# Layer 0's experts take the context rows of four experts as one tile and the context units of both halves as one tile, and the first route and gather stand inside the routing stage

## The chip, the cores and the metric

One core of one Trainium2 chip runs the whole program. The metric is the device time of one execution in microseconds (us); lower is better. TensorE (PE) multiplies, VectorE (DVE) and ScalarE (ACT) split and move tiles, GpSimd (POOL) issues gathers and scatters, and SyncE (SP) issues nearly all other DMA transfers, in its program's order.

## The reference, cut to what matters

The model has two layers over 1024 latent tokens and 256 context tokens of width 1024. A layer has a mixer (layer 0 recurrent, layer 1 attention), an output projection, and then a mixture of 16 experts in which each expert chooses its tokens: 128 of the latents and, in layer 0 only, 32 of the context.

```python
def expert_choice_ffn(h, w_router, w_gate, w_up, w_down):
    B, T, _ = h.shape
    cap = CAP_FACTOR * T // N_EXPERTS
    aff = jax.nn.softmax((h @ w_router).astype(jnp.float32), axis=-1)
    g, idx = lax.top_k(jnp.swapaxes(aff, 1, 2), cap)
    ...
    xg = h[bidx, idx]
    hid = jax.nn.silu(jnp.einsum('becd,edf->becf', xg, w_gate)) * jnp.einsum('becd,edf->becf', xg, w_up)
    y = jnp.einsum('becf,efd->becd', hid, w_down) * g[..., None].astype(h.dtype)
    return jnp.zeros_like(h).at[bidx, idx].add(y)
```

## The kernel before, in words

Each layer ends in a `tail` (output projection by `mixed`, residual, router, and the choice of tokens) and then `experts`. Latent products are done in three fp32r matmuls (`mm3`, L138 to L140): each factor is split into a high part (ACT, L144) and a low part (DVE, L145). Weights come in chunks of 1 MB: `wc` is the raw chunk, `wch` and `wcl` its two parts. In layer 0 eight raw chunks fit: five in a ring, which earlier stages use for other weights too, and three spare ones; three pairs of `wch` and `wcl` fit. An expert uses twelve chunks: for each half of its 1024 hidden units two of w_gate and two of w_up (`gate_up`, called with q = 0 and 1), then four of w_down (`down`, q = 0 to 3).

Layer 0 does the context with the raw chunks in plain f32, four small matmuls at a time (`mm_context`, L1143). After the second chunk pair of a half it runs the half's context products (`cg<-wc,xct`, 16 instructions), and in `down` after q = 1 and after q = 3 the context products of two chunks (`cg<-wc,hct`, 8 instructions each). A raw chunk can be loaded over only after its context products. Ahead of the products, PE turns tiles by transposition: `xg` (latent rows, `prep`, L1195), `xgc` (32 context rows of this expert, L1203), `sil` (hidden units of a half, `turn`, L1266) and `hc` (context units of a half, L1272). ACT or DVE copy what was turned to `xct` and `hct`.

PE's order is set by hand; a scheduler orders the other engines by it. `rt_hot` and `rt_i` make the list of an expert's rows (`route`), POOL gathers them (`xg<-hl,rt_i`), and the results are added by a scatter (`xl<-ye,rt_i`). `pooled` and `gated` say how the low parts of a layer's first chunks are made: on POOL, or on DVE behind a small POOL instruction.

In `mixed`, `oc` are the mixer's rows, `owr` and `wo` the raw and split weights of the attention's output projection, `wr` the router's weights, `rg` three rows of modulation and gain for the router, `rx` the residual rows, and `m` and `nf` modulation rows. `wdr` are weights of layer 1, loaded early, and `fe` rows of layer 0's mixer.

Of the kernel before, what the change touches and what calls it, by code (L numbers as in the profile page):

```python
# [22 lines left out]
D = 1024  # L23
# [85 lines left out]

class Kernel:  # L110
# [7 lines left out]
    pooled, gated = (2, 0), (0, 2)  # L118
# [16 lines left out]
    def mm3(self, out, a, b, first, last, skip=False):  # L135

        mm = self.nc.tensor.matmul
        mm(out, a[0], b[0], start=first, stop=False, skip_group_check=skip)  # L138
        mm(out, a[0], b[1], start=False, stop=False, skip_group_check=skip)  # L139
        mm(out, a[1], b[0], start=False, stop=last, skip_group_check=skip)  # L140
# [137 lines left out]
    def mod_round(self, l, r, pool, psum, ptag, wtile=None, column=False, ctag="tp", width=2048, **small):  # L278
# [6 lines left out]
        for k in range(KT):  # L285
# [12 lines left out]
            yield 1.0 / per  # L298
# [593 lines left out]
    def router(self, l, i, pool, psum):  # L892
# [22 lines left out]
    def affinities(self, h, r, out, turned, wr, pool, psum):  # L915
# [167 lines left out]

    def top_context(self, aff, pool, psum):
# [67 lines left out]
    def experts(self, l, routes, hs, xs, m5s, ring, pool, psum):  # L1152
# [10 lines left out]

        def pick(e):

            picked[e] = self.route(e, *routes[0], pool, tp())
            xg = pool.tile([128, D], F32, name="xg", bufs=2)
            fetched = gather(hs[0], picked[e][0], xg)
            if early and self.gated[l]:
                one = pool.tile([128, 1], F32, name="one")  # L1170
                with self.tc.issue_after(fetched.ins):
                    nc.gpsimd.memset(one, 1.0)
                for raw, hi, lo in early:
                    nc.vector.scalar_tensor_tensor(lo, raw, one, hi, op0=OP.mult, op1=OP.subtract)
            xgc = None
            if two:
                if e == 0:
                    routes[1] = self.top_context(routes[1], pool, tp)
                xgc = pool.tile([32, D], F32, name="xgc", bufs=2)
                gather(hs[1], routes[1][0][:, e:e + 1], xgc)  # L1180
            return xg, xgc
# [7 lines left out]
        def prep(xg, xgc):  # L1189
# [9 lines left out]
            if not two:  # L1199
                return xt, None  # L1200
            p = tp()
            for k in range(KT):
                nc.tensor.transpose(p[:, 32 * k:32 * k + 32], xgc[:, 128 * k:128 * k + 128], self.ident[:32, :32])  # L1203
            xct = pool.tile([128, KT, 32], F32, name="xct", bufs=2)
            nc.scalar.activation(xct, p[:, :256].rearrange("p (k t) -> p k t", t=32), AF.Copy)
            return xt, xct
# [10 lines left out]
        def wide_gate_up(e, q, x, accs):  # L1217

            for m, w in enumerate((wg, wu)):
                _, hi, lo = early.pop(0) if early else wide_chunk(e, q, w)  # L1220
                for a in range(2):
                    k = 2 * q + a
                    for half in range(2):
                        o = slice(512 * half, 512 * half + 512)
                        self.mm3(accs[half][:, m], (x[0][0][:, k, :], x[0][1][:, k, :]), (hi[:, a, o], lo[:, a, o]),
                                 k == 0, k == KT - 1)

        def gate_up(e, half, q, x, acc, cg):
            xt, xct = x
            c = []  # L1230
            for m, w in enumerate((wg, wu)):
                c.append(early.pop(0) if early else gate_up_chunk(e, half, q, w))
# [5 lines left out]
            if q:  # L1238
                for kk in range(KT):
                    self.mm_context(cg, xct, [held[2 * (kk // 4) + m][0][:, kk % 4, :] for m in range(2)], kk)  # L1240
                held.clear()

        def both(acc):

            sc = pool.tile([64, 512], F32, name="sc", bufs=2)
            nc.scalar.activation(sc, acc[64:128, :], AF.Copy)
            nc.vector.tensor_add(sc, sc, acc[0:64, :])
            return sc

        def activate(acc, cg):  # L1250
# [3 lines left out]
            if not two:  # L1254
                return sil, None
            sc = both(cg)
            hc = pool.tile([64, 512], F32, name="hc", bufs=2)
# [841 lines left out]
```

## Time and profile before

| | |
|---|---|
| median of 3 runs | 3310.74 us (3307.7 to 3312.14) |
| profiled execution | 3311.28 us, span 3309.5 us |
| mean granted TensorE clock | 0.962 |
| layer 0 experts | about 1087 to 1884 us |
| layer 1 tail | about 2510 to 2680 us |
| layer 1 experts | about 2681 to 3245 us |

The span runs from the first to the last instruction, and the time has 1.8 us more around it. A stage counts where PE waits, or where it never waits: there, only less PE work helps. The mean busy share of a stage doesn't tell which of the two it is; the list of PE's waits does.

### The profile page before, as it was taken

How to read it: one execution, taken by the hardware profiler on the slowest of the kernel's cores; microseconds unless marked ns; L12 is line 12 of the kernel's file. 1: busy time of each engine (PE TensorE's matmuls, PEld its weight loads, DVE VectorE, ACT ScalarE, POOL GpSimd, SP SyncE). 2: the span in 40 equal slices, each digit the busy share in tenths (PEclk: the TensorE clock that was granted, in tenths of full speed). 3: DMA queues.
4: the chain of work that ended last, by engine and by line, in shares of the span. 5: the costliest groups of instructions: out<-in, count | busy, mean ns of one | idle time of the engine just before them, and what ended most of it. 6: DMA issues, size and time to landing. Idle time of an engine off the chain costs nothing.

```text
span 3309.5 us, 50386 instructions
## 1 busy us (share of the span) xinstructions
PE 3051.5 (92%) x19910; PEld 2382.1 (72%) x19910; DVE 2264.7 (68%) x3526; ACT 1683.3 (51%) x2405; POOL 683.7 (21%) x730
## 2 busy tenths in 40 slices
PE   5999989897897899999999899999998879999997
PEld 4878776686675566666666587888886658887775
DVE  4774463535657777777777676666665588988887
ACT  4444342635221556556566444555553247766675
POOL 3134461426211312212212110000000100111111
PEclk8999999999799899999999999999998979999999
DMA  6112144234764687887887712100106569999995
GB/s 212 47 31 63 41 133 154 57 90 151 243 211 133 235 292 266 286 296 263 286 295 266 253 55 49 30 23 22 26 9 229 188 235 379 373 358 368 367 358 183
DMA packets 252798, 624.92 MB, mean 189 GB/s; under 512 B 47876, under 2 KB 107482, under 8 KB 222866
## 3 DMA queue, kind: packets, MB, share of 16 engines
q1 hardware_dynamic: 227154, 545.17, 45.5%
q0 software_dynamic: 25408, 76.54, 8.3%
q8 instruction: 156, 2.56, 0.3%
q14 instruction: 80, 0.66, 0.1%
HBM read 560.71 MB, written 60.92 MB: 188 GB/s over the span
## 4 chain that ended last, share of the span: by engine, by line
PE 35%; issue 20%; DVE 5%; POOL 4%; ACT 3%; DMA 2%; SPq 0%; POOLq 0%; ACTq 0%; DVEq 0%
PE acc L139 7%; PE acc L140 7%; PE acc L138 7%; PE tp L138 2%; PE tp L139 2%; PE tp L140 2%; PE tp L1788 2%; POOL xl L1298 1%; POOL xc L1298 1%; DMA xl<-ye,rt_i 1%; POOL xg L1161 1%; PE s L1757 1%; PE s L138 1%; PE s L140 1%; PE s L139 1%
## 5 line engine op out<-in xcount | busy, mean ns | idle before, releaser
L145 DVE TENSOR_TENSOR wcl<-wc,wch 128x2048 fp32r<-128x2048 f32 x380 | 874.3, 2308 | 208.0 <-ACT wch L144 206.9
L144 ACT ACTIVATE wch<-wc 128x2048 fp32r<-128x2048 f32 x380 | 728.0, 1918 | 360.5 <-PE acc L140 317.3
L139 PE MATMUL acc<-wcl,xt 128*128 128x512 f32 x1024 | 408.5, 399 | 0.3 <-DVE wcl L145 0.3
L138 PE MATMUL acc<-wch,xt 128*128 128x512 f32 x1024 | 405.9, 404 | 1.8 <-ACT xt L144 1.8
L140 PE MATMUL acc<-wch,xt 128*128 128x512 f32 x1024 | 406.8, 398 | 0.0
L138 PEld LDWEIGHTS acc<-wch,xt 128*128 128x128 f32 x1024 | 194.5, 190 | 72.5 <-issue 25.1
L140 PEld LDWEIGHTS acc<-wch,xt 128*128 128x128 f32 x1024 | 193.9, 189 | 45.4
L139 PEld LDWEIGHTS acc<-wcl,xt 128*128 128x128 f32 x1024 | 194.3, 190 | 43.5 <-DVE wcl L145 0.7
L139 PE MATMUL acc<-wcl,ht 128*128 128x512 f32 x512 | 206.7, 404 | 8.1 <-DVE wcl L145 8.1
L138 PE MATMUL acc<-wch,ht 128*128 128x512 f32 x512 | 209.0, 408 | 0.4 <-ACT wch L144 0.4
L140 PE MATMUL acc<-wch,ht 128*128 128x512 f32 x512 | 202.8, 396 | 0.0
L1298 POOL DMA_INDIRECT xl<-ye,rt_i x31 | 103.1, 3326 | 457.8 <-DVE ye L1297 457.8
L138 PE MATMUL mm<-ahi,w 128*128 128x512 f32 (+1 forms) x480 | 182.6, 380 | 0.0
L139 PE MATMUL mm<-alo,w 128*128 128x512 f32 (+1 forms) x480 | 173.2, 361 | 0.0
L140 PE MATMUL mm<-ahi,w 128*128 128x512 f32 (+1 forms) x480 | 173.1, 361 | 0.0
L1161 POOL DMA_INDIRECT xg<-hl,rt_i x32 | 75.4, 2356 | 400.6 <-issue 176.1
L138 PE MATMUL mm<-w,ahi 128*128 128x256 f32 (+1 forms) x480 | 148.5, 309 | 2.5 <-DVE tm L432 2.5
L144 ACT ACTIVATE pt<-tp 128x512 fp32r<-128x512 f32 (+1 forms) x192 | 98.3, 528 | 101.9 <-PE tp L1788 100.7
L145 DVE TENSOR_TENSOR pt<-tp,pt 128x512 fp32r<-128x512 f32 (+1 forms) x192 | 113.7, 594 | 44.5 <-ACT pt L144 44.3
L140 PE MATMUL mm<-w,alo 128*128 128x256 f32 (+1 forms) x480 | 137.8, 287 | 0.0
L139 PE MATMUL mm<-w,ahi 128*128 128x256 f32 (+1 forms) x480 | 137.7, 287 | 0.0
L138 PE MATMUL acc<-wo,ot 128*128 128x512 f32 x288 | 120.2, 417 | 5.1 <-ACT wo L144 5.1
(530 smaller groups left out, 7090.1 us busy)
## 6 DMA issues: line engine op xcount, KB each, us to landing
wc<-in_w_gate SPq DMA_DIRECT2D x128, 1024.0 KB, 7.4
wc<-in_w_up SPq DMA_DIRECT2D x128, 1024.0 KB, 8.8
wc<-in_w_down SPq DMA_DIRECT2D x128, 1024.0 KB, 8.2
w<-in_w_mod SPq DMA_DIRECT2D x32, 1024.0 KB, 5.3
craw<-in_w_in SPq DMA_DIRECT2D x40, 256.0 KB, 3.1
wm<-in_w_mod SPq DMA_DIRECT2D x8, 1024.0 KB, 10.1
wc<-in_w_mod SPq DMA_DIRECT2D x8, 1024.0 KB, 10.3
xl<-rxm POOLq DMA_DIRECT2D x16, 512.0 KB, 5.5
```

What stands on the lines that cost most here:

```text
L138: mm(out, a[0], b[0], start=first, stop=False, skip_group_check=skip)
L139: mm(out, a[0], b[1], start=False, stop=False, skip_group_check=skip)
L140: mm(out, a[1], b[0], start=False, stop=last, skip_group_check=skip)
L144: self.nc.scalar.activation(hi, src, AF.Copy)
L145: self.nc.vector.tensor_sub(lo, src, hi)
L1161: return nc.gpsimd.indirect_dma_start(out=out, out_offset=None, in_=src, in_offset=bass.IndirectOffsetOnAxis(ap=idx, axis=0))
L1298: nc.gpsimd.indirect_dma_start(out=rows[i], out_offset=bass.IndirectOffsetOnAxis(ap=idx, axis=0), in_=y, in_offset=None, compute_op=OP.add)
L1757: nc.tensor.matmul(out, qrl[:, q], krs[:, ks], start=False, stop=True)
L1788: nc.tensor.transpose(p[:, 128 * j:128 * j + 128], pr[:, 128 * (t0 + j):128 * (t0 + j) + 128], self.ident)
```

## The change

1. Layer 0's context rows of four experts are gathered into one tile `xgc` of 128 rows, and turned once for four experts (`prep_context`, eight full transpositions, two ACT copies to `xct`).
2. `hc` is one tile of 128 partitions that holds the context units of both halves (and zeros). It is turned once for an expert by four full transpositions and one DVE copy (`turn_context`), instead of twice by four small ones.
3. `down` runs all its context products (16 instructions) behind the last latent product of q = 3, so the four raw w_down chunks are held until then.
4. Layer 0's first two chunks get their low parts on DVE behind a small POOL instruction (`gated`), not on POOL (`pooled`); in layer 1 `pooled` and `gated` are as before.
5. Expert 0's route and gather are issued inside the last context tile's `affinities` (`begin`); its rows go into a ring chunk. The choice of the context's tokens and four context gathers (`choose_context`) stand between gate and up of expert 0's first chunk pair.
6. `wr` and the first `rg` are loaded at the start of `mixed`, in both layers.
7. A round of modulation (`mod_round`) in layer 0's tail takes one step for a chunk, not two.
8. In layer 1's experts the hidden units are turned inside the next expert's `gate_up`, no longer inside `down`.
9. `owr` has its eight staging tiles set aside first, and the split weights are 16 tiles (`Rows`), not two.

```diff
-    pooled, gated = (2, 0), (0, 2)
+    pooled, gated = (0, 0), (2, 2)
...
-            yield 1.0 / per
+            if k % per == per - 1:
+                yield 1.0
...
             nc.sync.dma_start(rows[8 * j:8 * j + 8, :], src.rearrange("(k p) -> k p", p=128))
+        yield None
         p = psum("rl")
...
+        if amid:
+            amid()
...
+    def first_rows(self, picked, src, pool):
+
+        nc = self.nc
+        xg = self.ring_chunk(self.ring)[:, :D]
+        fetched = nc.gpsimd.indirect_dma_start(out=xg, out_offset=None, in_=src,
+                                               in_offset=bass.IndirectOffsetOnAxis(ap=picked[0], axis=0))
+        return picked, xg, self.one_behind(fetched, pool)
...
+        def pick_context(e):
+
+            if e % 4 == 0:
+                four.append(pool.tile([128, D], F32, name="xgc", bufs=1))
+            gather(hs[1], routes[1][0][:, e:e + 1], four[-1][32 * (e % 4):32 * (e % 4) + 32, :])
...
+        def prep_context(xgc):
+            xct = pool.tile([128, KT, 128], F32, name="xct", bufs=1)
+            for half in range(2):
+                p = tp()
+                for j in range(4):
+                    k = 4 * half + j
+                    nc.tensor.transpose(p[:, 128 * j:128 * j + 128], xgc[:, 128 * k:128 * k + 128], self.ident)
+                nc.scalar.activation(xct[:, 4 * half:4 * half + 4, :], p.rearrange("p (k t) -> p k t", t=128), AF.Copy)
+            return xct
...
             if q:
+                if half == 0 and e % 4 == 0:
+                    turned_rows[0] = prep_context(four.pop(0))
...
+        def turn_context(hct):
+
+            p = tp()
+            for j in range(4):
+                nc.tensor.transpose(p[:, 128 * j:128 * j + 128], hc[:, 128 * j:128 * j + 128], self.ident)
+            src = p.rearrange("p (k h t) -> p h k t", h=4, t=32)
+            nc.vector.tensor_copy(hct.rearrange("p (h k) t -> p h k t", h=2), src[:, 1::2])
...
-            if two and q % 2:
-                for kk in range(4):
-                    self.mm_context(cy, hct, [held[kk // 2][:, kk % 2, 512 * m:512 * m + 512] for m in range(2)],
-                                    2 * q - 2 + kk)
+            if two and q == 3:
+                with self.tc.issue_after(latest.ins):
+                    for kk in range(KT):
+                        self.mm_context(cy, hct, [held[kk // 2][:, kk % 2, 512 * m:512 * m + 512] for m in range(2)],
+                                        kk)
                 held.clear()
...
+                        if e and q % 2 == 0:
+                            turn(q // 2, hid[q // 2], late)
...
-                    if e < NE and q % 2:
-                        turn(q // 2, hid[q // 2], ht, None)
+                    if e == NE - 1 and q % 2:
+                        turn(q // 2, hid[q // 2], ht)
...
+        self.wr = self.router_weights(l, pool)
+        routed = self.router(l, tiles[0][0], pool, psum)
+        next(routed)
         ready = fetch(*tiles[0][:2], pool, psum)
...
+        def begin():
+
+            if l == 0 and found and not begun:
+                begun.append(self.first_rows(self.route(0, found[0], pay, mc, psum("tp")), self.hd[0], mc))
...
-                    wo = [pool.tile([128, KT, D], F32R, name=f"wo{j}") for j in range(2)]
+                    tags = ("m2", "m4", "m3", "rh", "rx", "rx", "rxm", "rxm")
+                    staged = [pool.tile([128, D], F32, name="owr", tag=t, bufs=2 if "x" in t else 1) for t in tags]
+                    wo = [Rows([pool.tile([128, D], F32R, name=f"wo{j}{k}") for k in range(KT)]) for j in range(2)]
```

How this moves instructions is seen at three places. The first is PE in the middle of an expert of layer 0, from the last context products of gate and up to the first w_down chunk. Before it reads as follows.

```order
L1143 MATMUL cg<-wc,xct 32x512 x16
L1195 MATMUL tp<-ident,xg 128x128 x8
...
L1203 MATMUL tp<-ident,xgc 128x32 x8
...
L1266 MATMUL tp<-ident,sil 128x128 x4
L1272 MATMUL tp<-ident,hc 128x32 x4
...
L1143 MATMUL cg<-wc,hct 32x512 x8
```

In the changed kernel the same stretch, of an expert that doesn't begin a group of four, reads as follows; the lines left out are `mm3` matmuls and the eight pairs of `rt_hot`.

```order
L1173 MATMUL cg<-wc,xct 32x512 x16
L1246 MATMUL tp<-ident,xg 128x128 x8
...
L1313 MATMUL tp<-ident,sil 128x128 x4
L1321 MATMUL tp<-ident,hc 128x128 x4
...
L1173 MATMUL cg<-wc,hct 32x512 x16
```

The transpositions of `xgc` are gone from this expert, those of `hc` are full and stand once, and the `hct` products are one block of 16 after all four w_down chunks.

The second place is SP at the start of layer 0's experts. Before, gate, up and gate chunks of expert 0 stood among the loads of the output projection (and two more a little later).

```order
L897 DMA rg<-in_norm_ffn 8x128
L1124 DMA wc<-in_w_gate 128x4x512
L1124 DMA wc<-in_w_up 128x4x512
L1124 DMA wc<-in_w_gate 128x4x512
L1473 DMA oc<-ocat 128x1024
L1124 DMA wc<-in_w_up 128x4x512
```

In the changed kernel the first weight chunk stands behind twenty loads of `wdr`, shown here from the last of them.

```order
L1591 DMA wdr<-in_w_dkv 128x256
L1154 DMA wc<-in_w_gate 128x4x512
L851 DMA m_10944<-mods 128x1024
L1529 DMA m5c<-mods 64x1x512
L1154 DMA wc<-in_w_up 128x4x512
L1154 DMA wc<-in_w_gate 128x4x512
```

So all chunks of expert 0 now start to load when the choice of tokens is nearly over. The third place is SP at the start of layer 1's tail. Before:

```order
L1491 DMA oc<-od 128x8x128
L847 DMA owr<-in_w_o 128x1024 x8
L1491 DMA oc<-od 128x8x128
L839 DMA m_23618<-mods 128x1024
L839 DMA m_23620<-mods 128x1024
L839 DMA m_23622<-mods 128x1024
L861 DMA nf<-in_norm_ffn 128x1024
L948 DMA wr<-in_w_router 128x8x16
L870 DMA rx<-xl 128x1024
L1491 DMA oc<-od 128x8x128
L897 DMA rg<-mods 8x128 x2
L897 DMA rg<-in_norm_ffn 8x128
```

And in the changed kernel:

```order
L963 DMA wr<-in_w_router 128x8x16
L909 DMA rg<-mods 8x128 x2
L909 DMA rg<-in_norm_ffn 8x128
L1556 DMA oc<-od 128x8x128
L859 DMA owr<-in_w_o 128x1024 x8
L1556 DMA oc<-od 128x8x128
L851 DMA m_23372<-mods 128x1024
```

`wr` and the three `rg` loads moved from behind `owr`, `m` and `rx` to ahead of the first `oc`.

## Rows read from the trace of the kernel before

**Rows 1.** The page's first part: busy time, share, instructions of each engine.

```profile
PE 3051.5 (92%) x19910; PEld 2382.1 (72%) x19910; DVE 2264.7 (68%) x3526; ACT 1683.3 (51%) x2405; POOL 683.7 (21%) x730
```

**Rows 2.** Busy time of PE, PEld, DVE, ACT, POOL, clock, DMA share, GB/s, 1200 to 1800.

```profile
1200.00:1800.00 600.00, 600.00 (x3403) 397.73 (x3405) 452.26 (x378) 359.57 (x292) 127.43 (x49) 1.00 0.82 280
```

**Rows 3.** Timeline of PE in layer 0's experts: start, duration, instruction (us).

```profile
1320.71 3.64 PE L1143 MATMUL cg<-wc,xct 128*32 128x512 f32 x32
1324.29 1.09 PE L1195 MATMUL tp<-ident,xg 128*128 128x128 f32 x8
1325.13 0.48 PE L138 MATMUL acc<-wch,ht 128*128 128x512 f32 x1
...
1326.62 0.40 PE L138 MATMUL acc<-wch,ht 128*128 128x512 f32 x1
1326.95 0.68 PE L1203 MATMUL tp<-ident,xgc 32*128 32x32 f32 x8
1327.56 0.50 PE L139 MATMUL acc<-wcl,ht 128*128 128x512 f32 x1
...
1329.35 0.43 PE L1272 MATMUL tp<-ident,hc 32*128 32x32 f32 x4
1329.71 0.50 PE L138 MATMUL acc<-wch,ht 128*128 128x512 f32 x1
...
1332.37 0.39 PE L140 MATMUL acc<-wch,ht 128*128 128x512 f32 x1
1332.69 1.92 PE L1143 MATMUL cg<-wc,hct 128*32 128x512 f32 x16
1334.54 0.51 PE L138 MATMUL acc<-wch,ht 128*128 128x512 f32 x1
...
1423.11 1.09 PE L1195 MATMUL tp<-ident,xg 128*128 128x128 f32 x8
```

**Rows 4.** DMA issues, 1320 to 1372: count, KB each, median us to landing.

```profile
wc<-in_w_up SPq DMA_DIRECT2D x4, 1024.0 KB, 12.0
```

**Rows 5.** Timeline of PE at the start of layer 0's tail.

```profile
882.93 1.12 PE L1484 MATMUL tp<-ident,oc 128*128 128x128 f32 x4 [3.92 <-DMA oc<-ocat]
```

**Rows 6.** Timelines of DVE, SP, POOL and PE, start of layer 0's experts.

```profile
1071.08 0.29 DVE L1053 TENSOR_TENSOR ch_slot<-ch_both 128x128 bf16<-128x128 f32 x1
1074.82 0.67 DVE L1073 TENSOR_TENSOR rt_hot<-slots,ch_slot 128x1024 bf16<-128x1024 bf16 x1
1081.67 9.18 DVE L145 TENSOR_TENSOR wcl<-wc,wch 128x2048 fp32r<-128x2048 f32 x1
1071.80 0.43 SPq L1526 DMA_DIRECT2D wdr<-in_w_kr  x1
1077.15 1.71 POOL L1161 DMA_INDIRECT xg<-hl,rt_i  x1 [4.40 <-DMA wdr<-in_w_dkv]
1087.57 1.09 PE L1195 MATMUL tp<-ident,xg 128*128 128x128 f32 x4 [5.31 <-DMA xg<-hl,rt_i]
1107.20 3.64 PE L1143 MATMUL cg<-wc,xct 128*32 128x512 f32 x32
```

**Rows 7.** Timeline of PE at the start of layer 1.

```profile
1901.56 1.47 PE L1562 MATMUL tp<-ident,x 128*128 128x128 f32 x4 [14.69 <-DVE x L1555]
```

**Rows 8.** Waits of PE, 2500 to 2690: us in total, times, longest.

```profile
PE rl L899 <- DMA rg<-in_norm_ffn: 6.5, 1, 6.5
PE acc L138 <- ACT wo L144: 5.1, 1, 5.1
```

**Rows 9.** Timeline of SP, and columns of rows 2 behind that wait.

```profile
2510.15 4.32 SPq L847 DMA_DIRECT2D owr<-in_w_o  x8
2529.88 3.95 SPq L897 DMA_DIRECT2D rg<-mods  x2
2538.40:2544.20 5.80, 5.72 (x15) 4.50 (x16) 4.28 (x8) 1.31 (x3) 1.12 (x2) 0.50 0.84 270
```

**Rows 10.** Waits of PE in layer 1's experts, 2690 to 3240.

```profile
PE acc L139 <- DVE wcl L145: 7.3, 9, 0.9
```

More of the change, by code (lines that the diff above doesn't have):

```diff
@@ L139, in mm3 @@
         mm(out, a[0], b[1], start=False, stop=False, skip_group_check=skip)
-        mm(out, a[1], b[0], start=False, stop=last, skip_group_check=skip)
+        return mm(out, a[1], b[0], start=False, stop=last, skip_group_check=skip)
     def split(self, hi, lo, src):
@@ L1082, in route, with one_behind @@
         return idx, g, s
+    def first_rows(self, picked, src, pool):
[4 more added lines that the diff above has]
+        return picked, xg, self.one_behind(fetched, pool)
+    def one_behind(self, issue, pool):
+        one = pool.tile([128, 1], F32, name="one")
+        with self.tc.issue_after(issue.ins):
+            self.nc.gpsimd.memset(one, 1.0)
+        return one
     def top_context(self, aff, pool, psum):
@@ L1162, in gather, with lows @@
                                                 in_offset=bass.IndirectOffsetOnAxis(ap=idx, axis=0))
+        def lows(one):
+            for raw, hi, lo in early:
+                nc.vector.scalar_tensor_tensor(lo, raw, one, hi, op0=OP.mult, op1=OP.subtract)
         def pick(e):
-            picked[e] = self.route(e, *routes[0], pool, tp())
+            if e == 0 and two:
+                picked[0], xg, one = routes[0][3]
+                lows(one)
+                return xg
+            picked[e] = self.route(e, *routes[0][:2], routes[0][2] if two else pool, tp())
@@ L1167, in pick @@
             xg = pool.tile([128, D], F32, name="xg", bufs=2)
             fetched = gather(hs[0], picked[e][0], xg)
[L1169 to L1180, printed above, removed]
@@ L1181, in pick, with choose_context @@
-            return xg, xgc
+            if early:
+                lows(self.one_behind(fetched, pool))
+            if two and e + 3 < NE:
+                pick_context(e + 3)
+            return xg
+        def pick_context(e):
+            if e % 4 == 0:
+                four.append(pool.tile([128, D], F32, name="xgc", bufs=1))
+            gather(hs[1], routes[1][0][:, e:e + 1], four[-1][32 * (e % 4):32 * (e % 4) + 32, :])
+        def choose_context():
+            routes[1] = self.top_context(routes[1], pool, tp)
+            for c in range(4):
+                pick_context(c)
@@ L1198, in prep @@
                 self.split(xt[0][:, s, :], xt[1][:, s, :], p.rearrange("p (k t) -> p k t", t=128))
[L1199 to L1206, printed above, removed]
+            return xt
         def gate_up_chunk(e, half, q, w):
@@ L1253, in activate, with turn @@
             nc.vector.tensor_mul(sil, sil, acc[:, 1])
[L1254 to L1257, printed above, removed]
-            nc.scalar.activation(hc[32:64, :], sc[0:32, :], AF.Silu)
-            nc.vector.tensor_mul(hc[32:64, :], hc[32:64, :], sc[32:64, :])
-            return sil, hc
-        def turn(half, hid, ht, hct):
-            sil, sc = hid
+            if two:
+                sc = both(cg, half)
+                h = hc[64 * half + 32:64 * half + 64, :]
+                nc.scalar.activation(h, sc[0:32, :], AF.Silu)
+                nc.vector.tensor_mul(h, h, sc[32:64, :])
+            return sil
+        def turn(half, sil, ht):
             p = tp()
@@ L1318, in experts @@
                     if e + 1 < NE:
[L1319 removed]
+                        x = prep(nxt)
                         if e + 2 < NE:
@@ L1423, in mixed @@
             yield 1.4
-        self.affinities(*late[1:-1], routers[late[0]], pool, psum)
+        self.affinities(*late[1:-1], routers[late[0]], pool, psum, amid if l == 0 else None)
         next(late[-1])
```

88 lines of the change are left out of this document (46 added, 42 removed).

## The prediction

> **What bounds the kernel now.** I read the page's engine list first [rows 1]: PE is busy 92% of the span, so most of a gain has to be PE work that goes away or a PE wait that ends sooner. Then I took the stages that the change touches one by one. In layer 0's experts PE is busy for all 600 us of a 600 us stretch at full clock, while DVE and ACT have some 150 and 240 us to spare and the DMA engines are busy 0.82 of the time [rows 2]; the list of PE's waits is empty there. This stage is PE's sum and nothing else. Two experts take 1423.11 - 1324.29 = 98.82 us, so one takes 49.41 [rows 3]. The other places are waits: at the start of layer 0's tail PE waits 3.92 us for `oc` [rows 5]; at the start of layer 0's experts 5.31 us for the gathered rows [rows 6]; at layer 1's start 14.69 us for `x`, behind the last expert's scatter [rows 7]; in layer 1's tail 5.1 us for `wo` and 6.5 us for `rg` [rows 8]. In layer 1's experts PE waits 7.3 us in all [rows 10].
>
> **A full expert of layer 0.** All durations are from the timeline of PE [rows 3], where twelve `mm3` matmuls start from 1329.71 to 1332.37, 0.24 us apart, and a change of shape costs about 0.1 on each side (1326.62 to 1326.95 is 0.33).
> - *Context rows.* Removed: eight small transpositions, 1326.95 to 1327.56, 0.61, with the changes of shape 0.8. Added once for four experts: eight full ones, for which `xg`'s eight stand (1324.29 to 1325.13, 0.84, with the changes 1.05, so 0.26 for an expert). The context products behind them wait for ACT's first copy, which only one matmul covers; I estimate 0.4 for a group of four, 0.1 for an expert. Saved: 0.44.
> - *Context units.* Removed: two blocks of four small ones, 0.36 each (1329.35 to 1329.71), no more than 0.05 of shape change since `sil` stands beside them: 0.8. Added: one block of four full, half of `xg`'s 0.84 and a change: 0.5. Saved: 0.3.
> - *Context products of w_down.* Removed: two blocks of eight, 1332.37 + 0.24 to 1334.54, 1.93 each and a change, 4.1 in all. Added: one block of sixteen, as the block of gate and up takes: 1320.71 to 1324.29, 3.58, and changes, 3.75. Saved: 0.3.
> - *What the middle block covered.* The second half of `ht` used to have two chunks and a context block between its transposition and its use, and now has one chunk (2.9), `rt_hot`'s block and the transpositions. On DVE it stands behind a 2.3 us split. I count 5.1 us until it is ready and 5.2 until it is wanted: a loss of 0 to 0.4, taken as 0.2.
>
> Sum: 0.44 + 0.3 + 0.3 - 0.2 = 0.84 for an expert, and with the first expert counted half (its start is below) 15.5 x 0.84 = 13 us. Bounds: 0.5 to 1.1, so 8 to 17. Of the freed time nothing else is waited for as long as the weights come in time (a rival below).
>
> The block of full transpositions is the place where a rule of the chip could matter. The rows put a transposition that moves 32 columns at 76 ns and one that moves 128 at 105 ns [rows 3]. The Trainium skill ("TensorE: Matmul & The Clock Gate", section "Back-to-back issue gap") gives an isolated matmul of up to 64 columns about 60 cycles and one of 128 columns 134, a ratio of 2.2 where these rows show 1.4. By that ratio the full ones would cost some 0.5 us more for an expert, an estimate from the page and the row, and the gain of the stage would shrink to about 5 us; the rows decide here, since they are of the same instructions.
>
> **Start of layer 0's experts.** Before, expert 0's list begins at 1074.82, though `ch_slot` stands ready at 1071.37: it queues behind the last context tile's affinities on DVE [rows 6]. With the first route ahead of them it begins about 1072, and I take the gather 2.5 us earlier, at 1074.7. It took from 1077.15 to 1087.57, 10.4 us, to arrive [rows 6], under a heavy DMA load that stays; so the rows arrive about 1085. DVE's 9.18 us split beside POOL's subtractions [rows 6], four times its usual 2.3, goes as well. Against this: no chunk of expert 0 is prefetched now. The first is issued at 1071.8 [rows 6] and the next three behind two `m5` rows, all in the burst that the gather shares; the fifth reuses the gathered rows' ring slot. And the choice of the context's tokens moves from a time in which PE waited anyhow to between PE's chunks: on DVE its third and fourth rounds, its casts and its copies stand ahead of the second chunk's low part, which I count to 16 us behind the rows' arrival. From there three chunks of 2.8 us and the context block of 3.6 bring the end of half 0 to 29 to 30 us behind the arrival, about 1114.5. Before, it is 1110.8 [rows 6]. So I take a **loss of 4 us**; bounds 3 gained (rows at 1080, every chunk landed) and 10 lost (chunks late and the clock slow for longer).
>
> **Start of layer 0's tail.** `wr` and three `rg` loads now stand ahead of `oc` on SP, each some 0.4 us of issue as SP's row of a small load shows [rows 6], and PE waits for this `oc` already [rows 5]: **1.9 lost**, bounds 0.8 and 2.5. The mod round's steps only change when the same matmuls run: nothing, and its loads stand ahead of the weight chunks as before.
>
> **End of layer 0.** The last latent product ends 2 us sooner, since the middle block of eight comes after it. `ye`, its scatter and the loads of `x` follow from it, and PE does nothing but wait for `x` [rows 7]: **2 gained**, bounds 0 and 2.1.
>
> **Layer 1's tail.** PE stops 6.5 us for `rg` [rows 8], whose loads SP issues only from 2529.88 on [rows 9]; now they are issued before `owr`, and 20 us old when PE asks. Behind the wait PE ran 5.8 us at clock 0.50 with 15 instructions [rows 9]: 1.2 GHz where 2.4 would have halved their time, about 2.6. What is late next is the residual chain (`m`, `nf`, `rx`), whose staging tiles are now freed by the first copies of `owr`, not the last ones; by its order on SP it lands some 5 us earlier and is wanted in the same tile, five k steps on, so it should be just covered. **9.1 gained**, bounds 3 and 9.1. `owr` itself, issued at 2510.15 [rows 9] when the attention's tiles are all free, now stands behind `wr`, which waits for a transposition of the attention's last block but one; it can go sooner by at most the 5.1 us that PE waits for `wo` [rows 8]. I take half, **2.5 gained**, bounds 0 and 5.1.
>
> **Layer 1's experts.** The turns move into a place where ACT and DVE have longer for them; the count of instructions is the same. Nothing but PE's 7.3 us of waits can go [rows 10]; I take **1 gained**, bounds 0 and 4.
>
> **Sum.** 13 - 4 - 1.9 + 2 + 9.1 + 2.5 + 1 = 21.7 us, from the profiled execution's 3311.3 to 3289.6; that execution lies 0.5 above the median of the runs, so **3289 us**.
>
> **The rivals.**
> - *A residual row takes the place of `rg` in layer 1's tail.* For it: the DMA engines were busy 0.84 there [rows 9], and `rx` is behind eight loads of weights on the same queue. Against it: its issue moves forward with its staging tiles. If PE stops as long for `rx` as for `rg`, the 9.1 go: 3298.
> - *Expert 0 starves.* For it: 8 MB of chunks which before were loaded in part during the output projection now come in one burst, in which a gather of 0.5 MB takes 10.4 us [rows 6]. The 10 us bound: 3295; with the clock slow through the first half 3300.
> - *Held chunks, the rival that ends slower.* All four w_down chunks are released at an expert's end, so the loads of the next expert's second half are issued then, the first of them 2.7 us ahead of the end. Its high part is wanted about 11.1 us behind the end, so it has to be there by 9: it may take 11.5 us. In a burst of four an `up` chunk took 12.0 [rows 4]; if the first of a burst takes as long as the last, PE stops 0.5 us in each expert, and 7.5 of the 13 go: 3296. At 2 us a stop it is slower than before: 30 lost, 3319; that decides from landings of about 13.5 us on. Against it: the first of a burst should land before the last, and the DMA engines have 0.18 to spare [rows 2].
> - *The freed PE time comes back as another engine's wait* (ACT's or DVE's splits): the first sum falls to 3 or less, 3299. Against it: DVE has 150 us to spare in 600 [rows 2].
>
> **How the numbers follow.** About 0.2%, 6.6 us, is what a measurement of this kernel can tell from no change. Chances: the forecast with its own bounds 0.58 (3281 to 3295); `rx` 0.14; expert 0 starved 0.12; held chunks mild 0.05, and strong enough to make it slower 0.05; PE time given back 0.06. All but the strong case lie below 3304 unless two of them meet, which I give 0.05 of their share. So faster 0.88, same 0.06, slower 0.06. The range goes from 3274 (every term near its upper bound but for the layer 1 experts) to 3304, which leaves out the strong case and a meeting of two.
>
> **What would show it.** In a middle expert: two starts of `xg`'s transpositions 48.4 to 48.7 us apart when no group begins between them, no PE wait there, `hct` products in one block of some 3.6 us, and chunk loads with landings under 11 us. At the start: the gather issued at 1073 to 1075 and half 0's context block ending 1108 to 1120. In layer 1's tail: no wait for `rg`, a wait for `wo` of 0 to 5 us. It is wrong if PE waits for `wch` or `wcl` in each expert of layer 0, or if a wait of 5 us or more for `rxm` stands where `rg`'s was.

## The result and the profile after

The kernel after takes 3281.7 us (median of 4 runs, 3278.04 to 3286.45), beside 3309.22 us of the kernel before on the same chip: a ratio of 0.9915, 95% interval 0.990 to 0.993. It is 27.5 us faster; 21.7 were forecast. Its profiled execution took 3282.35 us, span 3280.6, which is 28.9 less than the span of before. All time offsets below are of profiled executions: the start of a PE instruction in one kernel less the start of the same instruction in the other.

The page's list of engines and the row of the steady stretch answer to [rows 1, 2]:

```profile
PE 3024.6 (92%) x19750; PEld 2379.9 (73%) x19750; DVE 2265.1 (69%) x3512; ACT 1681.3 (51%) x2397; POOL 659.3 (20%) x724
```

```profile
1200.00:1800.00 600.00, 596.07 (x3371) 406.82 (x3368) 468.21 (x372) 369.35 (x294) 104.29 (x46) 1.00 0.84 293
```

PE still has the share of 92% that it had, with 27 us less of work. In layer 0's experts it now waits 4 us in 600. PE's timeline there answers to [rows 3]:

```profile
1374.05 1.09 PE L1246 MATMUL tp<-ident,xg 128*128 128x128 f32 x8
...
1377.79 0.60 PE L1313 MATMUL tp<-ident,sil 128*128 128x128 f32 x4
1378.23 0.62 PE L1321 MATMUL tp<-ident,hc 128*128 128x128 f32 x4
1378.60 0.48 PE L149 MATMUL acc<-wch,ht 128*128 128x512 f32 x1
...
1382.93 0.50 PE L151 MATMUL acc<-wch,ht 128*128 128x512 f32 x1 [0.31 <-DVE ht L156]
...
1388.27 3.64 PE L1173 MATMUL cg<-wc,hct 128*32 128x512 f32 x32
1391.84 0.50 PE L149 MATMUL acc<-wch,xt 128*128 128x512 f32 x1
```

These rows show the one block of full transpositions for the units, 0.37 us from 1378.23 to 1378.60, the one context block of w_down, 3.57 us, and a new short wait for `ht`. Over twelve experts (three groups of four) the starts of `xg` lie 47.90 us apart on the mean, 49.40 before: 1.50 saved per expert where 0.84 were forecast.

The start of layer 0's experts, with expert 0's half 0, answers to [rows 6] (PE, then POOL and DVE):

```profile
1085.13 1.97 PE L1246 MATMUL tp<-ident,wc 128*128 128x128 f32 x8 [6.75 <-DMA wc<-hl,rt_i]
1089.58 0.80 PE L149 MATMUL acc<-wch,xt 128*128 128x512 f32 x1 [2.48 <-ACT wch L1158]
1092.12 0.79 PE L150 MATMUL acc<-wcl,xt 128*128 128x512 f32 x1 [1.74 <-DVE wcl L1196]
1097.11 0.20 PE L1130 MATMUL tp<-ident,tf 16*32 16x16 f32 x1
1101.02 0.79 PE L150 MATMUL acc<-wcl,xt 128*128 128x512 f32 x1 [2.56 <-DVE wcl L1196]
1110.92 0.60 PE L1230 MATMUL tp<-ident,xgc 128*128 128x128 f32 x3 [2.36 <-DMA xgc<-hc,idx]
...
1111.75 0.63 PE L151 MATMUL acc<-wch,xt 128*128 128x512 f32 x1
1112.18 0.63 PE L149 MATMUL acc<-wch,xt 128*128 128x512 f32 x1
...
1117.66 3.64 PE L1173 MATMUL cg<-wc,xct 128*32 128x512 f32 x32
```

```profile
1076.52 1.39 POOL L1103 DMA_INDIRECT wc<-hl,rt_i  x1 [1.95 <-DVE rmx L951]
1097.79 0.94 POOL L1191 DMA_INDIRECT xgc<-hc,idx  x1 [18.57 <-DVE idx L1132]
```

```profile
1081.25 0.40 DVE L1125 MATCH_REPLACE8 affc<-tg,affc 16x256 f32<-16x256 f32 x1
1086.91 0.69 DVE L156 TENSOR_TENSOR xt<-tp,xt 128x512 fp32r<-128x512 f32 x1 [5.26 <-ACT xt L155]
1088.37 0.40 DVE L1123 MAX8 tg<-affc 16x8 f32<-16x256 f32 x1
1091.99 0.41 DVE L1123 MAX8 tg<-affc 16x8 f32<-16x256 f32 x1
```

Half 0's context block starts at 1117.66, 1107.20 before. DVE stood idle from 1081.65 to 1086.91, then did the third and fourth round of the context's choice between PE's chunks, so the gathers of context rows went out from 1097.79 on. Behind PE's wait for these rows the matmuls of 512 columns start 0.43 us apart up to 1114.31, where 0.23 is full speed (mean clock 0.67 from 1112 to 1116); so they do from 1101.90 to 1104.20, behind the wait for `wcl`. From 1100 to 1124 the kernel before has a clock of 1.00.

Layer 1's start answers to [rows 7] (PE first). Behind it stand POOL's last scatter and ACT's pass over the second tile of `x`, before and after:

```profile
1883.41 1.47 PE L1627 MATMUL tp<-ident,x 128*128 128x128 f32 x4 [10.42 <-DVE x L1620]
```

```profile
1883.17 1.56 POOL L1298 DMA_INDIRECT xl<-ye,rt_i  x1 [38.34 <-DVE ye L1297]
1898.47 1.06 ACT L1551 ACTIVATE junk<-x 128x1024 bf16<-128x1024 f32 x1 [1.42 <-DMA x<-xl]
```

```profile
1867.57 1.57 POOL L1348 DMA_INDIRECT xl<-ye,rt_i  x1 [40.30 <-DVE ye L1347]
1880.31 1.06 ACT L1616 ACTIVATE junk<-x 128x1024 bf16<-128x1024 f32 x1 [0.24 <-DMA x<-xl]
```

The pass began 15.3 us behind the start of the scatter before and 12.7 after. The waits of layer 1's tail answer to [rows 8]; the wait for `rg` is gone:

```profile
PE acc L149 <- ACT wo L155: 2.4, 1, 2.4
PE tp L936 <- DVE rxm L887: 2.1, 1, 2.1
```

The windows of the tail's second tile (columns as in [rows 2]) answer to the last row of [rows 9]:

```profile
2514.00:2518.00 4.00, 4.00 (x24) 3.36 (x22) 1.65 (x4) 1.53 (x3) 0.59 (x2) 1.00 0.97 283
2518.00:2522.00 4.00, 1.79 (x21) 1.09 (x20) 3.44 (x4) 1.54 (x3) 0.52 (x1) 0.86 0.97 372
2522.00:2526.00 4.00, 4.00 (x10) 3.12 (x10) 1.18 (x6) 0.40 (x2) 0.57 (x1) 0.50 1.01 355
```

PE was busy 1.79 of 4 us at the first tile's affinities, between short waits; then the granted clock was 0.50, which is 1.2 GHz, and ten matmuls filled 4 us, where 24 instructions fill them two rows above. Before, this clock came behind the wait for `rg`; now it comes behind the affinities.

| place | forecast (us) | gained (+) or lost (-), us |
|---|---|---|
| up to 875 us, which the change does not touch | 0 | +3.9 |
| start of layer 0's tail | -1.9 | -5.2 |
| start of layer 0's experts | -4 | -7.4 (-9.1 at the context block, 1.7 back behind it) |
| steady layer 0 experts, to the last context block's end | +13 | +22.6 |
| end of layer 0, to `x` | +2 | +4.3 |
| layer 1's tail, `wo` | +2.5 | +2.7 |
| layer 1's tail, `rg` | +9.1 | +8.1, then -4.1 |
| layer 1's experts | +1 | +1.4 |
| latents and attention, end | 0 | +2.6 |

Up to 875 us the program is the same in twelve kernels of this case, and their executions ended the stretch between 873.6 and 879.0 us. So the first row is scatter between executions, and other rows of that size, from one pair of executions, can hold as much of it.

### The profile page after: what moved, and what is told of

Its sections match the earlier page's. It is cut to its first block, busy times and chain, and to the rows that moved or that the text cites. A ratio compares the mean times of both kernels' runs of the same rounds, so it can differ in the third digit from the quotient of the medians.

```text
span 3280.6 us, 49970 instructions
## 1 busy us (share of the span) xinstructions
PE 3024.6 (92%) x19750; PEld 2379.9 (73%) x19750; DVE 2265.1 (69%) x3512; ACT 1681.3 (51%) x2397; POOL 659.3 (20%) x724
## 4 chain that ended last, share of the span: by engine, by line
PE 51%; DVE 5%; issue 5%; ACT 3%; DMA 2%; POOL 1%; POOLq 0%; ACTq 0%; SPq 0%; DVEq 0%
PE acc L151 11%; PE acc L150 10%; PE acc L149 10%; PE cg L1173 4%; PE tp L149 2%; PE tp L150 2%; PE tp L151 2%; PE tp L1853 2%; DVE wcl L156 2%; ACT wch L155 1%; DMA xl<-ye,rt_i 1%; PE tp L1246 1%; PE s L1822 1%; PE s L149 1%; PE s L151 1%
```

## The experiments

**Where does the unforecast part of the steady gain come from?** In the kernel before, the successive gate and up matmuls (512 columns) start 0.232 us apart, in the kernel after 0.227; spacings here are medians of the differences of starts inside chunks in PE's timeline, over 1150 to 1860 us for layer 0 and 2580 to 3200 for layer 1. These matmuls are not in the change. But its new list of tiles puts `xt` elsewhere: in the compiled programs' tables of addresses (not in the traces), layer 0's `xt0` stands at byte 141472 of a partition before and at 121632 after, where the weights `wch` begin at 72480 in both. Modulo 256 that is 160 before, 32 after, and 32 for the weights. Theory A is that this offset sets the spacing; rival B is that the other instructions do. Both kernels got 128 unused bytes on each side of `xt`:

```diff
-            xt = [pool.tile([128, KT, 128], F32R, name=f"xt{j}", bufs=1) for j in range(2)]
+            gap = pool.tile([128, 32], F32, name="gap", bufs=1) if two else None
+            xt = [pool.tile([128, KT, 128], F32R, name=f"xt{j}", bufs=1) for j in range(2)]
+            gap2 = pool.tile([128, 32], F32, name="gap2", bufs=1) if two else None
```

> The kernel after, with 128 unused bytes ahead of layer 0's xt0 and 128 behind xt1, so that the turned rows stand at address 121760 instead of 121632 and every tile behind them where it stood modulo 256; no instruction is added, removed or reordered. Theory A (the gate and up matmuls became faster, 226.7 ns apart where they were 232, because in the kernel after the stationary rows xt and the streamed weights stand at the same offset modulo 256 bytes): the spacing goes back to 231 to 233 ns, 96 x 5.5 ns = 0.53 us per expert, and the time rises by 8 to 10 us to about 3291. Rival B (the spacing fell because fewer other instructions, writes and small transposes stand among the matmuls): spacing 226.7, time within 3 us of the kernel after, 3282.

> The kernel before with the same 128 + 128 unused bytes round layer 0's xt tiles, which here brings them to the weights' offset modulo 256 (141600 for 141472); nothing else is touched. Theory A (placement): gate and up matmuls at 226.7 ns instead of 232, 0.5 us per expert, 8 to 9 us less in all, about 3301 us; the difference that is left to the kernel after is then about 19 us, what the instruction changes are worth by themselves. Rival B (instruction stream): 3309, no change within 3 us.

The spacings went to 232 in the first and to 227 in the second. PE's timelines of the kernel after and then of the first run show it, over 24 steps:

```profile
1299.72 0.39 PE L149 MATMUL acc<-wch,xt 128*128 128x512 f32 x1
...
1305.16 0.39 PE L149 MATMUL acc<-wch,xt 128*128 128x512 f32 x1
```

```profile
1300.26 0.39 PE L149 MATMUL acc<-wch,xt 128*128 128x512 f32 x1
...
1305.84 0.40 PE L149 MATMUL acc<-wch,xt 128*128 128x512 f32 x1
```

That is 5.44 us against 5.58. The mean period is 48.34 (after with moved `xt`, +0.44) and 48.90 (before with moved `xt`, -0.50). Times: 3285.18, ratio 0.9924 (0.9911 to 0.9937), span 5.3 us above the kernel after; and 3301.99, ratio 0.9972 (0.9963 to 0.9982), 10 us below the kernel before. Theory A holds, by the spacing in both directions and by the time of the second run; about 8 of the 22.6 us in the steady stretch are placement, by no intent of the change. In the first run the time rose less than A said: the period gave 0.44 and not 0.53, 7 us in all, and the interval overlaps that of the kernel after, so its time alone would not show it.

The next runs put every stationary operand of the experts at that offset, and in another kernel the mixer's `w` and layer 0's `ot`:

```diff
+            gap = pool.tile([128, 40], F32, name="gap", bufs=1) if not two else None   # ahead of xt
+            gap3 = pool.tile([128, 48], F32, name="gap3", bufs=1) if two else None    # behind hct
```

> The kernel after, with 192 unused bytes ahead of layer 0's ht tiles' region and 160 ahead of layer 1's xt tiles, so that all stationary operands of both layers' experts stand at the weights' offset modulo 256; no instruction changes. Theory A: layer 0's down matmuls go from 233 to 227 ns (48 x 16 x 6.5 ns = 5 us) and layer 1's, all 144 per expert, from 234 to 227 (144 x 16 x 7.5 ns = 17 us): 3260 us. Theory A with a bound by transfers in layer 1 (DMA share 0.96 there while PE runs): the 5 us of layer 0 come, in layer 1 PE waits for weights instead: 3270 to 3277, with waits for wch and wcl in layer 1 that grow from about 9 us to 15 to 25. Rival B: 3282 within 3 us, spacings as before.

```diff
             self.dt = pa.tile([128, NT, 16], F32, name="dt")
+            self.unused = pa.tile([128, 32], F32, name="gap")
```

> The kernel after with 128 unused bytes behind the tile dt, which brings the weights w of layer 0's mixer and the turned rows ot of layer 0's tail from offset 160 to offset 32 modulo 256, that of the rows ahi and of wo. Theory A, if it holds beyond the experts: 480 matmuls of wo 5 ns closer each, 2.4 us; some 2900 matmuls of the mixer, half of 512 and half of 256 columns, 3 to 5 ns closer each, 9 to 14 us where PE binds them, so 3266 to 3275 (ratio 0.987 to 0.9895). Rival: the mixer's spacing (232 and 119 ns) has another reason, and the time falls by the 2.4 us at most (ratio 0.9905 to 0.992).

The experts' run: 3267.96 us, ratio 0.9868 (0.9854 to 0.9883), some 15 us below the kernel after. Layer 1's spacing fell from 234 to 227, and its experts took 13 us less. Layer 0's for `ht` fell from 234 to 227 as well, but by 4.7 ns on the mean, which took the period from 47.90 to 47.70, 3 us and not the 5 expected. Layer 1 is not held by its transfers: its list of waits has 7.4 us for `wcl` where the kernel after has 7.3 (and the kernel before, [rows 10]), and the DMA share rose with PE's pace (kernel after, then this one):

```profile
2700.00:3200.00 500.00, 492.57 (x2275) 398.54 (x2274) 443.07 (x311) 351.08 (x247) 75.91 (x27) 1.00 0.96 366
```

```profile
2700.00:3200.00 500.00, 491.32 (x2320) 406.04 (x2319) 452.91 (x318) 358.39 (x251) 105.68 (x28) 1.00 0.98 373
```

The mixer's run: medians at 512 columns went from 231 or 232 to 227, those at 256 columns from 119 to 120: no gain there. The span fell 5.7 us (7 to 16 were expected, with a gain at 256 columns), the median of the runs only to 3280.01, ratio 0.9913 (0.9898 to 0.9928), which can't be told from the kernel after.

**The start of layer 0's experts.** The choice of the context tokens was moved ahead of the turning of expert 0's rows:

```diff
-        x = prep(pick(0))
+        xg = pick(0); choose_context(); x = prep(xg)
...
-            gate_up(e, 0, 0, x, *a0, choose_context if e == 0 else None)
+            gate_up(e, 0, 0, x, *a0)
```

> The kernel after, with the choice of the context tokens called ahead of the turning of expert 0's rows instead of between its first and second weight chunk; no instruction is added or removed. Theory C (the start of layer 0's experts lost about 9 us against the kernel before because rounds 3 and 4 of the choice, its small transpose at 1097 and so the gathers of the four experts' context rows stood behind expert 0's rows, and PE then waited until 1115 for those rows): the rounds run in VectorE's idle stretch 1081 to 1087, the gathers go out 6 to 10 us earlier, the wait of 2.4 us for xgc goes, and half 0's context block ends at 1112 to 1116 instead of 1121: 5 to 8 us faster, 3274 to 3277. Rival D (the loss is the arrival of the first weights and of expert 0's rows, which bind PE whatever stands between): within 2 us of the kernel after.

```profile
1081.00 0.20 PE L1130 MATMUL tp<-ident,tf 16*32 16x16 f32 x1 [6.04 <-ACT tf L1127]
1082.71 1.09 PE L1246 MATMUL tp<-ident,wc 128*128 128x128 f32 x4 [1.50 <-DMA wc<-hl,rt_i]
1084.48 0.79 PE L149 MATMUL acc<-wch,xt 128*128 128x512 f32 x1 [0.69 <-ACT xt L155]
1102.72 3.76 PE L1173 MATMUL cg<-wc,xct 128*32 128x512 f32 x32
```

The context block starts at 1102.72 instead of 1117.66, of which 2.4 were gained ahead of this place: 12.5 us, more than theory C's 5 to 8, and rival D falls. PE waits for the choice while the rows arrive, and loses nothing by it. Yet the time is 3278.59, ratio 0.9909 (0.9896 to 0.9922). The tiles of the choice are now made ahead of `xt` and push it to offset 96; the spacing went to 235 (on the mean to 233, from 228) and 0.5 us per expert was lost again, 8 us in all. Both together:

```diff
+        xg = pick(0); choose_context(); x = prep(xg)
...
+            gap = pool.tile([128, 48 if two else 40], F32, name="gap", bufs=1)   # ahead of xt
```

> The kernel after with the choice of the context tokens ahead of expert 0's rows (as in the run that moved it, which won 11 us at the start and lost 8 again because the tiles of the choice pushed xt to another offset) and with unused bytes that put xt and ht of both layers at the weights' offset modulo 256. Theory A with C: period in layer 0 47.45, half 0's context block ends near 1108, layer 1's spacing 227 to 228.5: 16 + 11 = 27 us below the kernel after, 3255 (ratio 0.983 to 0.984). Rival: the two overlap, because the earlier start of the experts is taken back where the chunks of weights arrive: 3262 to 3268 (0.9855 to 0.987).

It took 3257.36 us, ratio 0.9841 (0.9828 to 0.9855), period 47.70, the context block at 1105.65: the two add up, and this is the best kernel of the study, some 25 us below the kernel after.

**The parts of an expert, one undone at a time.** First the order of w_down's context product:

```diff
-            if two and q == 3:
-                with self.tc.issue_after(latest.ins):
-                    for kk in range(KT):
+            if two and q % 2:
+                with nullcontext():
+                    for kk in range(4):
...
-                                        kk)
+                                        2 * q - 2 + kk)
```

> The kernel after, with the context product of w_down in two blocks of four contraction steps again, not held behind the last latent matmul; everything else, every address too, as in the kernel after. The prediction gave this part 0.3 us per expert: the period goes from 47.63 to about 47.9, the time up by 4 to 6 us, ratio 0.9925 to 0.9935. Rival G (the one block only moves the same work to the end of the expert, and no change of the blocks' number is seen in the period): 47.6 to 47.7, same time within 2 us.

The period fell to 47.78, 0.12 below the kernel after: the part costs time. Its run took 3280.66, ratio 0.9914 (0.990 to 0.9927). PE's list of waits from 1150 to 1880 is empty here, where the kernel after has one row:

```profile
PE acc L151 <- DVE ht L156: 5.5, 15, 0.8
```

So the wait for `ht`, 0.37 per expert, takes back more than the one block saves (0.25, by difference): neither the forecast's +0.3 nor rival G. The times don't tell this run from the kernel after; the period does.

```diff
-                    nc.tensor.transpose(p[:, 128 * j:128 * j + 128], xgc[:, 128 * k:128 * k + 128], self.ident)
+                nc.tensor.transpose(p[:, 32 * k:32 * k + 32], xgc[:, 128 * k:128 * k + 128], self.ident[:32, :32])
...
-            four.append(pool.tile([128, D], F32, name="xgc", bufs=1))   # one for four experts
+            four.append(pool.tile([32, D], F32, name="xgc", bufs=2))    # one for each
```

> The kernel after, with the context rows of each expert gathered and turned for itself again (32 rows, eight transpositions of 32 columns, one ACT copy) in place of one tile for four experts; the units, w_down's block and every offset modulo 256 stay. The prediction gave this part 0.44 us per expert: period 48.3 where the kernel after has a mean of 47.89, and 0 to 2 us won back at the start, where one gather of 32 rows is waited for and not four: about 3287, ratio 0.9925 to 0.9935. If this part carries what is left of the measured 1.0 to 1.2 us per expert beyond the units' 0.3: period 48.6 to 48.8, ratio 0.994 to 0.996.

```diff
-            turn_context(hct)
...
+                    nc.tensor.transpose(p[:, 32 * j:32 * j + 32], hc[half][32:64, 128 * j:128 * j + 128],
+                                        self.ident[32:64, 32:64])   # in turn(), for each half
```

> The kernel after, with the context units of each half turned for themselves again (two blocks of four transpositions of 32 columns) in place of one block of four for both halves; rows, w_down's block and every offset modulo 256 stay. The prediction gave this part 0.3 us per expert: period 48.2 where the kernel after has a mean of 47.89, about 3286, ratio 0.9925 to 0.9935. If the wait for ht (0.37 us per expert in the kernel after) is covered by the block that now stands behind each half's transpositions: period 47.8 to 48.0, time unchanged within 2 us.

Periods 48.55 and 48.49: the rows are worth 0.65 and the units 0.59 per expert, where 0.44 and 0.3 were forecast. In the second the wait for `ht` stayed at 4.3 us in all, so the rival that it would be covered falls. Times 3287.77, ratio 0.993 (0.9917 to 0.9944), and 3289.06, ratio 0.9928 (0.9915 to 0.9942). PE's timeline with rows per expert shows the price of the small block:

```profile
1324.15 0.40 PE L149 MATMUL acc<-wch,ht 128*128 128x512 f32 x1
1324.57 0.68 PE L1225 MATMUL tp<-ident,xgc 32*128 32x32 f32 x8
1325.18 0.50 PE L150 MATMUL acc<-wcl,ht 128*128 128x512 f32 x1
1325.51 0.40 PE L151 MATMUL acc<-wch,ht 128*128 128x512 f32 x1
```

From 1324.15 to 1325.51 less two spacings of 0.233 is 0.89.

**The start of layer 0's tail.** First only the router's loads went back, then also the steps of the modulation round:

```diff
-        self.wr = self.router_weights(l, pool)
+        self.wr = self.router_weights(l, pool) if l else None     # in layer 0 behind mod_rows again
...
-                        if n > 1:
+                        if n > 1 or l == 0:
```

> The kernel after, with layer 0's loads of the router (wr, and rg of the first tile) issued where the kernel before issued them; layer 1 keeps them early. Theory E (the start of layer 0's tail, which lost 5.2 us where 1.9 were predicted, lost them because the four loads stand on SP ahead of the first oc loads): the wait for oc goes from 6.3 back to about 4 us, the waits and the half clock at tile 0's affinities near 917 to 924 us go, and the time falls by 3 to 5 us against the kernel after (ratio to the kernel before 0.990 to 0.9905 where after has 0.9915). Rival F (those 3 us come from where the modulation products now stand, a part that this kernel keeps): 0 to 2 us, with the wait for rht still there.

```diff
-            if k % per == per - 1:
-                yield 1.0
+            yield 1.0 / per
```

> The kernel after, with layer 0's router loads where the kernel before issued them and the steps of the modulation rounds yielded after each contraction step again, as in the kernel before; so the start of layer 0's tail is that of the kernel before. Rival F of the run on the router loads (the small waits and the half clock at tile 0's affinities, 917 to 924 us, come from where the modulation products now stand): the 5.2 us lost between 875 and 925 come back nearly all, offset to the kernel before at the first chunk of choices -3 to -4 us where the kernel after has +1.3, and the time falls 3 to 5 us (ratio 0.990 to 0.9905). Otherwise (they depend on when the residual chain lands): the wait for rht of some 4 us stays, ratio 0.991 within 0.0007.

The first: 3278.1, ratio 0.9903 (0.9888 to 0.9918). The wait for `oc` fell from 6.3 to 3.8, but the wait for `rht` at the affinities rose from 2.0 to 4.1, and PE stood 0.6 us later there than in the kernel after, counted from where the wait for `oc` begins. The second: 3277.87, ratio 0.9898 (0.9883 to 0.9913), with PE 7.0 us ahead of the kernel after at the fourth tile by the same count, and 4.5 at the choice's first matmul (`rl<-ch_cmp`). The windows 918 to 926 of the kernel after and of this one show the clock:

```profile
918.00:926.00 8.00, 7.73 (x35) 5.61 (x36) 3.20 (x10) 0.78 (x3) 0.00 (x0) 0.66 0.01 2
```

```profile
918.00:926.00 8.00, 8.00 (x45) 6.09 (x44) 4.90 (x7) 2.24 (x4) 2.42 (x4) 1.00 0.36 122
```

The intervals of the two runs and the kernel after overlap, so the runs alone don't settle it; the traces speak for rival F. The longest wait for `rht` is 1.1 to 4.1 us in all eleven kernels with the new steps, and 0.3 in the three with the old ones (the kernel before, it with `xt` moved, and this run). How much it costs is less sure than the 5.2 of the table: from where the wait for `oc` begins to that matmul, eight kernels with the new start of the tail took 154.8 to 157.9 us, 156.1 on the mean, and the three with the old steps 152.8 to 154.8, 153.7 on the mean. That is 2.4 lost; the kernel after and the kernel before stand at the two ends.

**All together.** The kernel with both improvements, with w_down's context in two blocks and the bytes behind `dt`; its diff is the sum of those above.

> The kernel with both improvements (context choice first, xt and ht of both layers at the weights' offset) and two more edits: the context product of w_down in two blocks, which took 0.12 us off an expert's period, and 128 unused bytes behind dt, which brought the mixer's w and layer 0's ot to offset 32 modulo 256. If the four add up: 16 x 0.12 = 2 us and 2 to 6 us below the run with both improvements (ratio 0.9841), so a ratio of 0.9815 to 0.983, 3249 to 3254 us. If the block order only trades a wait for ht against a change of shape once the matmuls are closer: 0.983 to 0.984.

It took 3263.43, ratio 0.9858 (0.9838 to 0.9878): 6 us above the run without the two small edits and above both expectations; the two intervals still overlap at their ends. The period did fall (47.64). The loss stands elsewhere, at the end of the mixer; the windows are of the kernel with both improvements, and of this one:

```profile
820.00:840.00 20.00, 19.32 (x429) 12.29 (x417) 10.80 (x32) 2.97 (x10) 5.38 (x6) 0.91 0.92 329
```

```profile
820.00:840.00 20.00, 19.48 (x362) 12.48 (x360) 9.17 (x26) 2.64 (x8) 4.16 (x5) 0.64 0.81 303
840.00:860.00 20.00, 19.37 (x358) 12.84 (x353) 9.89 (x28) 3.74 (x10) 6.52 (x8) 0.76 0.51 166
```

PE lost 8 us from 826 on while busy nearly all the time, at a mean granted clock of 0.64 and then 0.76 (0.50 from 826 to 846); all four runs had a mean clock of 0.958 to 0.961, those of the kernel with both improvements 0.962 to 0.964. Why the clock fell there in this kernel and not with the bytes behind `dt` alone stays open.

## Why the prediction was right, and where its terms were off

The direction and the range held, and PE's work in layer 0's experts was the largest term, as forecast. No rival came: no `rxm` wait of 5 us (2.1), chunk loads that landed in 7 to 9 us (medians, 1320 to 1372) where 13.5 would have decided, and no PE wait for weights in a steady expert. The mechanisms of the steady experts, of `rg` and of `wo` were right; several sizes were not. In the profiled pair the places that the change touches add up to 22.4 us beside the 21.7 of the forecast, and that is luck: the steady experts gave 9.6 more and the end of layer 0 2.3 more, the two starts lost 6.7 more, and `rg` kept 5.1 less. The other 6.5 stand in places that the change does not touch.

- *Steady experts, 13 forecast, 22.6 measured.* About 8 of the difference is the address offset of `xt`, which no step of the prediction had; "a full expert" assumed that untouched matmuls keep their spacing. The instructions alone are worth 49.40 - 0.50 - 47.90 = 1.00 per expert, against 0.84. Inside, three terms were mis-sized. *Context rows* 0.44: 0.65, since a small block costs 0.89 and not 0.8, and the 0.1 of waiting for ACT's copy did not come (a group's first period is 1.04 longer, the block alone). *Context units* 0.3: 0.59; the full block stands right behind `sil` and costs 0.37, where I took 0.5 with a change of shape, which leaves 0.48 for each of the two small ones, where I took 0.4. *Context products of w_down*, 0.3 less the 0.2 for what the middle block covered: -0.12, since the wait for `ht` was 0.37, at the far end of its bounds. The three sum to 1.12; the spacing of `ht` was 232 before and 234 after, which is 0.1 over an expert's 48 matmuls and would be the rest, but no run shows it by itself. The Trainium skill's gap ratio of 2.2 between 128 and 64 columns ("TensorE: Matmul & The Clock Gate", section "Back-to-back issue gap") is not seen here: four full transpositions took 0.37, four small ones 0.36 [rows 3]. The prediction's estimate from that ratio was also too large: 65 ns more for each of the six full ones of an expert is 0.4 us, not 0.5.
- *Start of layer 0's experts, 4 lost forecast, 7.4 measured.* The rows arrived at 1085, as worked out, though the gather went out at 1076.5, later than the 1073 to 1075 named, and the second chunk's low part was there 16 us behind them, as worked out too. The end of half 0 was put at 1114.5 and came at 1121.3. What the sum left out stands in between: four gathers behind the second cast and PE's wait of 2.4 us for them until 1110.92, and the two spells at half the clock, some 2.5 us together; the prediction had the clock only in its bound. The moved choice is the cause: with it ahead of the rows the context block began 72 to 75 us behind the choice's first matmul in three kernels, where the kernel before and its copy with `xt` moved took 75 and 77, and the kernel after 85.
- *Start of layer 0's tail, 1.9 lost forecast, 5.2 measured.* The wait for `oc` grew by 2.4, near the 1.9 (four loads of the row's 0.43 are 1.7). The step that failed is "the mod round's steps only change when the same matmuls run: nothing": with them the affinities' wait and 8 us at a lower clock appeared, and went with the old steps. Over all kernels the start lost 2.4 and not 5.2, so the forecast's size was near and part of the 5.2 is scatter.
- *End of layer 0, 2 forecast, 4.3 measured.* 1.7 came as worked out, since the last latent product ends ahead of the context block. The other 2.6 lie behind the scatter, outside the bounds of 0 to 2.1: `x` was there sooner. The loads of the context's `x` now go out 1.8 us behind those of the latents, 0.95 before; whether that is why was not tried.
- *`wo`, 2.5 and 2.7; layer 1's experts, 1 and 1.4*: as worked out. For `wo` the forecast was half of the wait, for want of more, so its hit is chance.
- *`rg`, 9.1 forecast, 4.0 kept.* The wait went and 8.1 came, but the 2.6 of the clock (half of the 5.8 is 2.9) were counted as won for good. The clock fell at the next thin place, the affinities, and cost 4.1. That this would have come before too, had `rg` been there in time, was not tried.

## What to carry to other kernels

A change in a pool's list of tiles moves the tiles behind it: ahead of a forecast, compare the addresses of the matmuls' operands in both programs, and after a result, the spacing of matmuls that were not touched. A choice on another engine goes where PE waits anyhow, not between its first chunks. A wait that ends ahead of a thin stretch of PE may give the clock's share back there, so a clock term should be counted only up to the next such stretch.

## What the runs showed of the hardware

The spacing of fp32r matmuls of 512 columns goes with the offset of the stationary tile modulo 256 bytes: 227 ns where it was 32, that of the streamed operand, and 232 to 235 (medians) at 96, 128 and 160. Matmuls of 256 columns (119 to 120) and the f32 context products (98 on the mean) did not move with it. All streamed tiles of the moved pairs stood at 32. The 32 of the stationary tile is not enough by itself: in layer 1 of both kernels `wqh` stands at 32 and its streamed `cqt` at 160, and these come 232 apart, while `ot` and `wo`, both at 32, come 227 apart. That speaks for equal offsets; no long stream has them equal elsewhere than at 32, so it stays open. One pair contradicts either rule: the scores of layer 1 (`kt`, `qt`, both at 32) come 231 to 234 apart. What in the memory makes the difference was not tried.
